# A hybrid encoder layer on one core: the second gate tile in another PSUM ring, the third weight in the extra staging tile, and block products with the summed index innermost

## The chip, the cores and the metric

The kernel runs on one core of a Trainium2 chip. The metric is the device time of one execution in microseconds. Before the change it is 937.7 us, the median of 3 runs (935.88 to 937.9). The core has a matrix engine (PE, with its weight loads shown apart as PEld), a vector engine (DVE), a scalar engine (ACT), GpSimd (POOL) and an engine that here only issues transfers (SP). Each engine works through its own list of instructions in order and waits where an operand isn't there yet.

## The reference

One layer on 512 tokens of width 1024. All inputs are float32.

```python
h = rms_norm(x, attn_norm_g[l])
(a_q, a_ckv, a_iq, a_ik, a_iw, s5_u, c_qkv, c_z, c_a, c_b,
 gates) = jnp.split(h @ w_in[l], split_points, axis=-1)
y_a = dsa_attention(...) @ w_proj_a[l]      # top-k sparse attention over a shared latent
y_b = s5_branch(...) @ w_proj_b[l]          # complex diagonal state space layer, then a GLU
y_c = gdn_branch(c_qkv, c_z, c_a, c_b, ...) @ w_proj_c[l]
g_a, g_b, g_c = jnp.split(jax.nn.sigmoid(gates), N_BRANCH, axis=-1)
x = x + (g_a * y_a + g_b * y_b + g_c * y_c) @ w_out[l]
x = x + conv_glu_ffn(rms_norm(x, ffn_norm_g[l]), w_up[l], ffn_conv_w[l], w_down[l])
return rms_norm(x, final_norm_g)
...
# in gated_delta_rule, in chunks of 64 tokens, 4 heads
m = jnp.where(strict, jnp.einsum('bhncd,bhnsd->bhncs', kb, k) * decay, 0.0)
rhs = jnp.concatenate([v * beta[..., None], kb * jnp.exp(gam)[..., None]], axis=-1)
sol = lax.linalg.triangular_solve(m + eye, rhs, left_side=True, lower=True, unit_diagonal=True)
```

The unit triangular system is solved per head and per chunk of 64 tokens.

## The kernel before

The input projection is cut into column tiles of 128, each an output of 128x512 (channels by tokens) summed over eight 128-row slices. Every float32 operand is split into a rounded part and its remainder, named h and l, and every slice is three matmuls: h by h, h by l and l by h. So one weight tile of 128x1024 feeds 24 matmuls of 128x512. A weight tile passes through three steps: a load into a staging tile w (SP, L280), a cast on ACT that makes wh (L256), and a subtraction on DVE that makes wl (L257). There are two normal staging tiles; a third one, w3, is there for some stretches, the start among them, and `wload` gives it to one load in three, by a counter `wi`.

PSUM is cut into rings of 128x512 tiles: "acc" has 2, "sm" 2, "pt" 3 and "po" 1. A matmul that starts a tile waits until the tile's former content has been read.

At the start the program loads x transposed (xt) in eight slices, splits it, and multiplies it by the first four weight tiles of the state space input: the first two into "acc", the other two into "pt". It also loads x as it is (sq) and sums its squares on ACT for the norm. Then h is scaled and split (hh, hl), and the projections follow in the order of a list. The first two gate tiles are made by `proj_pair`, slice by slice in turn, while h comes in slices; every gate is drained by a tanh on ACT (m_th, L1324) and sent to memory (gd, L1325).

The delta rule (`gdn_main`) makes for each head the matrix NT and inverts the unit triangular blocks of 64 as follows. The 32x32 diagonal blocks are sent through memory so that each of 128 partitions holds one block (g_ND, L942 to L946). The 16x16 diagonal blocks are inverted by substitution on DVE (L949, L950), and the off-diagonal 16x16 block is two products of 16x16 matrices: one with the off-diagonal part of g_ND, one with the inverse X2. Each product is four times a multiplication into a tile of 128x512 (L958) and a sum over its innermost index (L959). ACT and DVE copy the result into Xa and Ya (L961 to L968); these go to memory (g_xd, L972, L973) and come back as g_X (by SP) and g_Y (by POOL's queue, L980), block diagonal. PE multiplies g_X into g_NT; DVE masks the result into g_P (L998); PE multiplies that with g_Y, and so on for the other 32x32 halves.

The program is written stage by stage, with generators that let projections and stages take turns. The order of the instructions on each engine is set afterwards by a scheduler of the framework, from an estimate of its own; so a small edit can move instructions far from it. After the delta rule comes the sparse attention, the merge with the gates, the output projection and the gated MLP.

Of the kernel before, what the change touches and what calls it, by code (L numbers as in the profile page):

```python
# [13 lines left out]
OP = mybir.AluOpType  # L14
# [29 lines left out]
def _bc(ap, axis, n):  # L44
    a = ap.unsqueeze(axis)
    shape = list(a.shape)
    shape[axis] = n
    return a.broadcast_to(shape)
# [177 lines left out]
class _K:  # L226
# [46 lines left out]
    def wload(self, src, n=1024, hl=None, extra=False):  # L273
        nc = self.nc
        self.wi += 1
        if self.w3 and self.wi % 3 == 0:
            w = self.w3.tile([128, 1024], F32, tag="w3", name="w", bufs=1)
        else:
            w = self.wp.tile([128, 1024], F32, tag="w", name="w", bufs=2)
        nc.sync.dma_start(w[:, :n], src)  # L280
        if hl is None:
            if self.wx and extra:
                hl = [self.wx.tile([128, 1024], F32R, tag="x" + z, name="w" + z, bufs=1) for z in "hl"]
            else:
                hl = [self.wp.tile([128, 1024], F32R, tag="w" + z, name="w" + z, bufs=self.wb) for z in "hl"]
        h, l = hl
        if self.gpw and GP and self.wi % GP == 0:
            nc.scalar.copy(h[:, :n], w[:, :n])
            nc.gpsimd.tensor_tensor(l[:, :n], w[:, :n], h[:, :n].bitcast(F32), OP.subtract)
        else:  # L290
            self.split(h[:, :n], l[:, :n], w[:, :n])
        return h, l
# [57 lines left out]
    def proj_pair(self, i):  # L350

        self.ahead(2)
        two, pss = [self.fq.pop(0) for _ in range(2)], [self.acc(), self.acc()]
        assert [q[0] for q in two] == [i, i + 1]
        self.lasta, self.lastv = two[1][2:]
        for k in range(8):
            c = slice(k * 128, k * 128 + 128)
            for ps, q in zip(pss, two):
                wh, wl = q[1]
                self.mm(ps, wh[:, c], self.hh[:, k], k == 0, False)  # L360
                self.mm(ps, wl[:, c], self.hh[:, k], False, False)
                self.mm(ps, wh[:, c], self.hl[:, k], False, k == 7)
        self.ahead(3)
        return pss
# [451 lines left out]
    def gdn_main(self):  # L816
        nc = self.nc
        tt = nc.vector.tensor_tensor
# [36 lines left out]
        for h in range(4):  # L855
            for z, src in ((0, self.kT), (1, self.qT)):
                ps = self.gp()
                for t in range(4):
                    c = slice(t * 128, (t + 1) * 128)
                    self.tr(ps[:, c], src[:, h, c])  # L860
                dst = k_t[:, h]
                if z == 0:
                    nc.vector.tensor_copy(dst, ps)
                for t in range(4):
                    c = slice(t * 128, (t + 1) * 128)
                    jk = self.g2.tile([128, 128], F32, tag="jk", name="g_jk", bufs=2)
                    j = z * 16 + t * 4 + h
# [32 lines left out]
        for h in range(4):  # L900
            t2 = lambda nm: self.g2.tile([128, 512], F32, tag="t2", name="g_" + nm)
            p1, p2 = self.gp(), self.gp()
            for t in range(4):
                c = slice(t * 128, (t + 1) * 128)
# [3 lines left out]
            for i, x, y in ((h, self.kT, KB), (4 + h, self.qT, QD)):  # L908
# [4 lines left out]
                for t in range(4):  # L913
                    c = slice(t * 128, (t + 1) * 128)
# [10 lines left out]
            for t in range(4):  # L925
                c = slice(t * 128, (t + 1) * 128)
# [5 lines left out]
        lo, up, h0_, h1_ = slice(0, 64), slice(64, 128), slice(0, 16), slice(16, 32)  # L932
        ND = self.g2.tile([128, 2, 16, 16], F32, tag="t2", name="g_ND")
        W = self.g2.tile([128, 1024], F32, tag="S", name="g_W", bufs=1)
        w3 = lambda a, b, n: W[:, a:b].rearrange("p (i k) -> p i k", k=n)
        X, X2, X1, T1, X21 = w3(0, 256, 16), w3(256, 512, 16), w3(512, 640, 8), w3(640, 768, 8), w3(768, 896, 8)
        tmp = self.g2.tile([128, 512], F32, tag="t2", name="g_xt")
        Xa = self.g2.tile([128, 16, 32], F32, tag="t2", name="g_Xa")
        Ya = self.g2.tile([128, 16, 32], F32, tag="t2", name="g_Ya")
        nc.gpsimd.memset(Xa[lo, :, h1_], 0.0)  # L940
        nc.gpsimd.memset(Ya[up, :, h0_], 0.0)
        nc.sync.dma_start(ND[lo, 0], nv[:, h0_, h0_])  # L942
        nc.sync.dma_start(ND[up, 0], nv[:, h1_, h1_])
        nc.sync.dma_start(X.rearrange("p a b -> p (a b)"), self.I["const"][:, CC["eye16"][0]:CC["eye16"][1]])
        nc.sync.dma_start(ND[lo, 1], nv[:, h0_, h1_])
        nc.sync.dma_start(ND[up, 1], nv[:, h0_, h1_])  # L946
        for i in range(1, 16):
            tv = tmp[:, :i * i].rearrange("p (a b) -> p a b", a=i)
            tt(tv, X[:, 0:i, 0:i], _bc(ND[:, 0, 0:i, i], 2, i), OP.mult)  # L949
            nc.vector.tensor_reduce(X[:, i, 0:i], tv.rearrange("p j k -> p k j"), AX.X, OP.add)  # L950
        nc.vector.tensor_copy(X1[lo], X[lo, :, 0:8])
        nc.scalar.copy(X1[up], X[lo, :, 8:16])
        nc.scalar.copy(X2[lo], X[up])
        nc.scalar.copy(X2[up], X[up])
        t4 = tmp.rearrange("p (i k j) -> p i k j", i=4, k=8)
        for dst, a, b in ((T1, ND[:, 1].rearrange("p j i -> p i j"), X1), (X21, X2, T1)):
            for c in range(0, 16, 4):
                tt(t4, _bc(a[:, c:c + 4], 2, 8), _bc(b.rearrange("p j k -> p k j"), 1, 4), OP.mult)  # L958
                nc.vector.tensor_reduce(dst[:, c:c + 4], t4, AX.X, OP.add)  # L959
        tr_ = lambda x: x.rearrange("p i k -> p k i")  # L960
        nc.scalar.copy(Xa[lo, :, h0_], X[lo])  # L961
        nc.scalar.copy(Xa[up, :, h1_], X[up])
        nc.scalar.copy(Ya[lo, :, h0_], tr_(X[lo]))
        nc.scalar.copy(Ya[up, :, h1_], tr_(X[up]))
        nc.vector.tensor_copy(Xa[up, :, 0:8], X21[lo])
# [18 lines left out]
        for h0 in (0, 2):  # L984
# [5 lines left out]
            with self.tc.issue_after(self.lastm[2].ins):  # L990
                for h in range(2):
                    for t in range(4):
                        c = slice(t * 128, (t + 1) * 128)
# [7 lines left out]
            for h in range(2):  # L1001
                for t in range(4):
                    c = slice(t * 128, (t + 1) * 128)
# [38 lines left out]
        for t in range(4):  # L1042
            c = slice(t * 128, (t + 1) * 128)
# [40 lines left out]
        for h in range(4):  # L1084
# [3 lines left out]
            for t in range(4):  # L1088
                c = slice(t * 128, (t + 1) * 128)
# [608 lines left out]
```

## Time and profile before

| | |
|---|---|
| time, median of 3 runs | 937.7 us (935.88 to 937.9) |
| profiled execution | 937.33 us, its span 935.5 us |
| PE busy | 914.2 us, 98% of the span |
| DVE busy | 646.1 us, 69% |
| ACT busy | 414.4 us, 44% |
| mean granted clock of PE | 0.992 of full speed |
| data moved | 114.55 MB, 122 GB/s over the span |

The profiled execution is 0.37 us under the median. Busy PE means that a matmul is in flight; matmuls overlap, so the pace of a stretch is read from start to start and not from the duration of one. The granted clock is the share of 2.4 GHz that PE had; its other level is 1.2 GHz. A bracket at the end of a row of a timeline is the idle time of the engine before that instruction and what ended it.

### The profile page before, as it was taken

Reading aid. Unit: us, or ns where it says so; the run is one execution under the profiler, and the core shown is the slowest. Engines: PE = TensorE matmul, PEld = TensorE weight load, DVE = VectorE, ACT = ScalarE, POOL = GpSimd, SP = SyncE. Lnnn points to the kernel's source line nnn. Section 1 sums busy time; section 2 is a strip of 40 time slices with the busy share of each in tenths; the row PEclk is TensorE's granted clock in tenths of the full one; section 3 lists DMA queues with packets and bytes.
Section 4 is the critical chain, followed back from the end, with each engine's and each line's share of the span. In section 5 each row is a group of like instructions: output and inputs, shape, how many; then the busy total and the mean of one; then the engine's idle time right before and its main releaser. Section 6 shows DMA issues by size and latency. Waiting matters only on the chain.

```text
span 935.5 us, 12723 instructions
## 1 busy us (share of the span) xinstructions
PE 914.2 (98%) x4804; PEld 744.2 (80%) x4804; DVE 646.1 (69%) x1136; ACT 414.4 (44%) x753; POOL 62.7 (7%) x103
## 2 busy tenths in 40 slices
PE   8989999999999999899999999999999999999996
PEld 6768877788887778788777889888888888888885
DVE  6988498989999779467768545866666666522423
ACT  7467454244575634258733224534443443321212
POOL 3121001021003200400100000000000000000000
PEclk9999999999999999899999999999999999999999
DMA  9585323342335644631147513423223323232312
GB/s 341 179 208 150 105 95 114 119 147 90 101 103 136 166 119 150 191 124 37 45 135 234 205 46 113 136 90 110 94 90 100 103 90 94 87 113 91 103 55 90
DMA packets 48269, 114.55 MB, mean 122 GB/s; under 512 B 13712, under 2 KB 15120, under 8 KB 48080
## 3 DMA queue, kind: packets, MB, share of 16 engines
q1 hardware_dynamic: 40144, 96.76, 32.0%
q0 software_dynamic: 4032, 9.97, 4.4%
q10 hardware_dynamic: 4032, 7.01, 2.1%
q8 instruction: 38, 0.62, 0.3%
q14 instruction: 23, 0.19, 0.1%
HBM read 94.84 MB, written 14.42 MB: 117 GB/s over the span
## 4 chain that ended last, share of the span: by engine, by line
PE 84%; DVE 9%; issue 3%; DMA 2%; ACT 1%; SPq 1%; POOL 0%; POOLq 0%; DVEq 0%; ACTq 0%
PE ps_acc L248 43%; PE ps_sm L248 22%; PE ps_pt L248 13%; PE ps_po L248 4%; DVE wl L257 1%; PE ps_pt L251 1%; DMA sq<-in_x_dram 1%; PE ps_sm L251 1%; DMA w<-in_w_glu_dram 1%; DVE g_xt L958 1%; DVE g_W L959 1%; DVE a_p L1256 0%; DVE s_rd L710 0%; DVE ht L1491 0%; DVE hl L257 0%
## 5 line engine op out<-in xcount | busy, mean ns | idle before, releaser
L257 DVE TENSOR_TENSOR wl<-w,wh 128x1024 fp32r<-128x1024 f32 (+1 forms) x140 | 168.9, 1207 | 137.7 <-ACT wh L256 137.4
L256 ACT CAST wh<-w 128x1024 fp32r<-128x1024 f32 (+1 forms) x140 | 145.5, 1040 | 231.2 <-PE ps_acc L248 126.5
L248 PE MATMUL ps_acc<-hh,wh 128*128 128x512 f32 x376 | 151.2, 402 | 3.4 <-ACT m_th L1324 2.9
L248 PE MATMUL ps_acc<-hh,wl 128*128 128x512 f32 x376 | 150.4, 400 | 0.0
L248 PE MATMUL ps_acc<-hl,wh 128*128 128x512 f32 x376 | 149.2, 399 | 0.0
L248 PEld LDWEIGHTS ps_acc<-hh,wh 128*128 128x128 f32 x376 | 70.9, 188 | 21.4 <-ACT m_th L1324 3.3
L248 PEld LDWEIGHTS ps_acc<-hh,wl 128*128 128x128 f32 x376 | 71.0, 189 | 17.5 <-issue 1.2
L248 PEld LDWEIGHTS ps_acc<-hl,wh 128*128 128x128 f32 x376 | 70.9, 189 | 16.8 <-issue 1.1
L248 PE MATMUL ps_acc<-f_hh,wh 128*128 128x512 f32 x160 | 62.3, 389 | 0.0
L248 PE MATMUL ps_acc<-f_hl,wh 128*128 128x512 f32 x160 | 62.3, 389 | 0.0
L248 PE MATMUL ps_acc<-f_hh,wl 128*128 128x512 f32 x160 | 62.2, 389 | 0.0
L248 PE MATMUL ps_sm<-f_hh,wh 128*128 128x512 f32 x160 | 62.2, 389 | 0.0
L248 PE MATMUL ps_sm<-f_hl,wh 128*128 128x512 f32 x160 | 62.2, 389 | 0.0
L248 PE MATMUL ps_sm<-f_hh,wl 128*128 128x512 f32 x160 | 62.2, 389 | 0.0
L256 ACT CAST ah<-f_th 128x512 fp32r<-128x512 f32 x22 | 13.6, 620 | 57.6 <-DVE f_th L1629 57.6
L248 PEld LDWEIGHTS ps_sm<-f_hh,wh 128*128 128x128 f32 x160 | 30.1, 188 | 6.3
L248 PEld LDWEIGHTS ps_acc<-f_hl,wh 128*128 128x128 f32 x160 | 30.0, 188 | 6.3
L248 PEld LDWEIGHTS ps_sm<-f_hl,wh 128*128 128x128 f32 x160 | 30.0, 188 | 6.2
L248 PEld LDWEIGHTS ps_acc<-f_hh,wl 128*128 128x128 f32 x160 | 30.1, 188 | 6.2
L248 PEld LDWEIGHTS ps_acc<-f_hh,wh 128*128 128x128 f32 x160 | 30.0, 187 | 6.2
L248 PEld LDWEIGHTS ps_sm<-f_hh,wl 128*128 128x128 f32 x160 | 30.0, 187 | 6.2
L1627 ACT ACTIVATE f_th<-f_a 128x512 f32<-128x512 f32 x22 | 13.9, 632 | 45.2 <-DVE f_a L1624 45.2
(553 smaller groups left out, 1941.6 us busy)
## 6 DMA issues: line engine op xcount, KB each, us to landing
w<-in_w_in_dram SPq DMA_DIRECT2D x50, 512.0 KB, 3.5
w<-in_w_up_dram SPq DMA_DIRECT2D x44, 512.0 KB, 3.3
w<-in_w_down_dram SPq DMA_DIRECT2D x22, 512.0 KB, 3.3
gd<-m_th ACTq DMA_DIRECT2D x24, 256.0 KB, 2.1
m_th<-gd SPq DMA_DIRECT2D x24, 256.0 KB, 3.6
w<-in_w_out_dram SPq DMA_DIRECT2D x8, 512.0 KB, 3.9
sq<-in_x_dram SPq DMA_DIRECT2D x4, 512.0 KB, 9.0
w<-in_w_proj_b_dram SPq DMA_DIRECT2D x4, 512.0 KB, 3.8
```

The lines of the kernel that those rows point to most:

```text
L248: return self.nc.tensor.matmul(out, lhsT, rhs, start=start, stop=stop)
L251: return self.nc.tensor.transpose(out, in_, self.ident[base:base + n, base:base + n])
L256: self.lasta = nc.scalar.copy(hi, src)
L257: self.lastv = nc.vector.tensor_sub(lo, src, hi.bitcast(F32))
L958: tt(t4, _bc(a[:, c:c + 4], 2, 8), _bc(b.rearrange("p j k -> p k j"), 1, 4), OP.mult)
L959: nc.vector.tensor_reduce(dst[:, c:c + 4], t4, AX.X, OP.add)
L1627: nc.scalar.activation(th, tl[0], AF.Tanh)
```

## The change

There are three edits. `wload` gives the extra staging tile to the loads with `wi % 3 == 2` instead of 0. `proj_pair` takes its second tile from the "pt" ring. And the block products keep X1 and T1 transposed, with a transposed copy of the off-diagonal part of g_ND (NDt) that ACT makes in half of the tile Ya, so that both operands of each multiplication have the summed index innermost.

```diff
--- before.py
+++ after.py
@@ -273,7 +273,7 @@
     def wload(self, src, n=1024, hl=None, extra=False):
         nc = self.nc
         self.wi += 1
-        if self.w3 and self.wi % 3 == 0:
+        if self.w3 and self.wi % 3 == 2:
             w = self.w3.tile([128, 1024], F32, tag="w3", name="w", bufs=1)
         else:
             w = self.wp.tile([128, 1024], F32, tag="w", name="w", bufs=2)
@@ -350,7 +350,7 @@
     def proj_pair(self, i):
 
         self.ahead(2)
-        two, pss = [self.fq.pop(0) for _ in range(2)], [self.acc(), self.acc()]
+        two, pss = [self.fq.pop(0) for _ in range(2)], [self.acc(), self.acc("pt")]
         assert [q[0] for q in two] == [i, i + 1]
         self.lasta, self.lastv = two[1][2:]
         for k in range(8):
@@ -933,33 +933,37 @@
         ND = self.g2.tile([128, 2, 16, 16], F32, tag="t2", name="g_ND")
         W = self.g2.tile([128, 1024], F32, tag="S", name="g_W", bufs=1)
         w3 = lambda a, b, n: W[:, a:b].rearrange("p (i k) -> p i k", k=n)
-        X, X2, X1, T1, X21 = w3(0, 256, 16), w3(256, 512, 16), w3(512, 640, 8), w3(640, 768, 8), w3(768, 896, 8)
+        X, X2, X21 = w3(0, 256, 16), w3(256, 512, 16), w3(768, 896, 8)
+
+        X1, T1 = w3(512, 640, 16), w3(640, 768, 16)
         tmp = self.g2.tile([128, 512], F32, tag="t2", name="g_xt")
         Xa = self.g2.tile([128, 16, 32], F32, tag="t2", name="g_Xa")
         Ya = self.g2.tile([128, 16, 32], F32, tag="t2", name="g_Ya")
         nc.gpsimd.memset(Xa[lo, :, h1_], 0.0)
-        nc.gpsimd.memset(Ya[up, :, h0_], 0.0)
         nc.sync.dma_start(ND[lo, 0], nv[:, h0_, h0_])
         nc.sync.dma_start(ND[up, 0], nv[:, h1_, h1_])
         nc.sync.dma_start(X.rearrange("p a b -> p (a b)"), self.I["const"][:, CC["eye16"][0]:CC["eye16"][1]])
         nc.sync.dma_start(ND[lo, 1], nv[:, h0_, h1_])
         nc.sync.dma_start(ND[up, 1], nv[:, h0_, h1_])
+        NDt = Ya.rearrange("p (z a) b -> p z (a b)", z=2)[:, 0].rearrange("p (i j) -> p i j", i=16)
+        nc.scalar.copy(NDt, ND[:, 1].rearrange("p j i -> p i j"))
         for i in range(1, 16):
             tv = tmp[:, :i * i].rearrange("p (a b) -> p a b", a=i)
             tt(tv, X[:, 0:i, 0:i], _bc(ND[:, 0, 0:i, i], 2, i), OP.mult)
             nc.vector.tensor_reduce(X[:, i, 0:i], tv.rearrange("p j k -> p k j"), AX.X, OP.add)
-        nc.vector.tensor_copy(X1[lo], X[lo, :, 0:8])
-        nc.scalar.copy(X1[up], X[lo, :, 8:16])
+        tr_ = lambda x: x.rearrange("p i k -> p k i")
+        nc.vector.tensor_copy(X1[lo], tr_(X[lo, :, 0:8]))
+        nc.scalar.copy(X1[up], tr_(X[lo, :, 8:16]))
         nc.scalar.copy(X2[lo], X[up])
         nc.scalar.copy(X2[up], X[up])
         t4 = tmp.rearrange("p (i k j) -> p i k j", i=4, k=8)
-        for dst, a, b in ((T1, ND[:, 1].rearrange("p j i -> p i j"), X1), (X21, X2, T1)):
+        for dst, a, b in ((tr_(T1), NDt, X1), (X21, X2, T1)):
             for c in range(0, 16, 4):
-                tt(t4, _bc(a[:, c:c + 4], 2, 8), _bc(b.rearrange("p j k -> p k j"), 1, 4), OP.mult)
+                tt(t4, _bc(a[:, c:c + 4], 2, 8), _bc(b, 1, 4), OP.mult)
                 nc.vector.tensor_reduce(dst[:, c:c + 4], t4, AX.X, OP.add)
-        tr_ = lambda x: x.rearrange("p i k -> p k i")
         nc.scalar.copy(Xa[lo, :, h0_], X[lo])
         nc.scalar.copy(Xa[up, :, h1_], X[up])
+        nc.gpsimd.memset(Ya[up, :, h0_], 0.0)
         nc.scalar.copy(Ya[lo, :, h0_], tr_(X[lo]))
         nc.scalar.copy(Ya[up, :, h1_], tr_(X[up]))
         nc.vector.tensor_copy(Xa[up, :, 0:8], X21[lo])
```

On SP the edit of the staging tile moves a load. The rows are the start of the program; w is a weight tile, xt and sq are x transposed and plain. Before:

```order
L1424 DMA xt<-in_xt_dram 128x1024
L280 DMA w<-in_w_in_dram 128x1024
L1424 DMA xt<-in_xt_dram 128x1024 x2
L1432 DMA sq<-in_x_dram 128x1024 x3
L280 DMA w<-in_w_in_dram 128x1024
L1432 DMA sq<-in_x_dram 128x1024
L1455 DMA ident<-in_const_dram 128x128
L280 DMA w<-in_w_in_dram 128x1024
```

After:

```order
L1428 DMA xt<-in_xt_dram 128x1024
L280 DMA w<-in_w_in_dram 128x1024
L1428 DMA xt<-in_xt_dram 128x1024 x2
L280 DMA w<-in_w_in_dram 128x1024
L1436 DMA sq<-in_x_dram 128x1024 x4
L1459 DMA ident<-in_const_dram 128x128
L280 DMA w<-in_w_in_dram 128x1024
```

The second of these loads of w, the third weight of the program, stood behind three loads of sq and stands ahead of all four now.

On PE the matmuls of the first gates move. The rows are the start of the pair, right behind the last matmuls of the index projection; hh, hl and wh, wl are the parts of h and of the weights. Before:

```order
L248 MATMUL ps_sm<-xh,wl 76x512
L248 MATMUL ps_acc<-hh,wh 128x512
L248 MATMUL ps_acc<-hh,wl 128x512
L248 MATMUL ps_acc<-hh,wh 128x512
L248 MATMUL ps_acc<-hl,wh 128x512
L248 MATMUL ps_acc<-hh,wh 128x512
L248 MATMUL ps_acc<-hh,wl 128x512
L248 MATMUL ps_acc<-hl,wh 128x512
L248 MATMUL ps_acc<-hh,wh 128x512
L248 MATMUL ps_acc<-hh,wl 128x512
L248 MATMUL ps_acc<-hl,wh 128x512
L248 MATMUL ps_acc<-hh,wl 128x512
```

After:

```order
L248 MATMUL ps_sm<-xh,wl 76x512
L248 MATMUL ps_acc<-hh,wh 128x512
L248 MATMUL ps_pt<-hh,wh 128x512
L248 MATMUL ps_acc<-hh,wl 128x512
L248 MATMUL ps_acc<-hl,wh 128x512
L248 MATMUL ps_acc<-hh,wh 128x512
L248 MATMUL ps_acc<-hh,wl 128x512
L248 MATMUL ps_acc<-hl,wh 128x512
L248 MATMUL ps_acc<-hh,wh 128x512
L248 MATMUL ps_acc<-hh,wl 128x512
L248 MATMUL ps_pt<-hh,wl 128x512
L248 MATMUL ps_pt<-hl,wh 128x512
```

Two tiles of "acc" take turns before. Now one of the pair is in "pt", and further matmuls into "acc", those of the third gate, follow among them from the next rows on.

On PE the cover of the inverse moves too. The rows are around the first products with g_X; f is the output of the state space layer, a_c and a_wk belong to the attention's keys. Before:

```order
L248 MATMUL ps_pt<-f_l,wh 128x512
L248 MATMUL ps_pt<-f_h,wl 128x512
L248 MATMUL ps_acc<-a_ch,a_wkl 128x512
L248 MATMUL ps_acc<-wh,a_ch 128x512
L248 MATMUL ps_acc<-wl,a_ch 128x512
L248 MATMUL ps_acc<-wh,a_cl 128x512
L248 MATMUL ps_sm<-g_X,g_NT 128x64 x8
L248 MATMUL ps_acc<-f_h,wh 128x512
```

After:

```order
L248 MATMUL ps_pt<-f_h,wl 128x512
L248 MATMUL ps_acc<-a_ch,a_wkl 128x512
L248 MATMUL ps_sm<-g_X,g_NT 128x64 x3
L248 MATMUL ps_acc<-wh,a_ch 128x512
L248 MATMUL ps_sm<-g_X,g_NT 128x64 x2
L248 MATMUL ps_acc<-wl,a_ch 128x512
L248 MATMUL ps_acc<-wh,a_cl 128x512
L248 MATMUL ps_sm<-g_X,g_NT 128x64 x3
L248 MATMUL ps_pt<-a_kd,a_qh 128x128
L248 MATMUL ps_pt<-a_kl_3705,a_qh 128x128
L248 MATMUL ps_pt<-a_kd,a_qh 128x256
L248 MATMUL ps_pt<-a_kl_3705,a_qh 128x256
```

From the last matmul with g_rows up to the first one with g_X there are 198 matmuls before and 215 now, and the products with g_Y follow those with g_X after four score products, where twelve and more matmuls stood between them before.

On DVE the split of the attention's weight (a_wkl, L257) stood ahead of the copies into Xa and Ya that end the inverse, and stands behind them now.

## Rows read from the trace of the kernel before

**Rows 1.** The page: busy time of each engine; chain of waits, shares of the span.

```profile
PE 914.2 (98%) x4804; PEld 744.2 (80%) x4804; DVE 646.1 (69%) x1136; ACT 414.4 (44%) x753; POOL 62.7 (7%) x103
...
PE 84%; DVE 9%; issue 3%; DMA 2%; ACT 1%; SPq 1%; POOL 0%; POOLq 0%; DVEq 0%; ACTq 0%
```

**Rows 2.** Windows: length; busy (count) of PE, PEld, DVE, ACT, POOL; granted clock, DMA, GB/s.

```profile
50.00:60.00 10.00, 7.15 (x25) 5.35 (x24) 10.00 (x17) 4.36 (x5) 1.52 (x4) 0.83 1.10 247
270.00:280.00 10.00, 10.00 (x50) 8.20 (x50) 10.00 (x21) 5.93 (x29) 0.00 (x0) 1.00 0.30 97
380.00:390.00 10.00, 8.12 (x31) 7.27 (x32) 1.57 (x4) 2.15 (x5) 8.69 (x9) 0.66 0.81 207
```

**Rows 3.** Waits of PE: what it waited for: total us, times, longest us.

```profile
PE ps_acc L248 <- ACT m_th L1324: 2.9, 1, 2.9
PE ps_sm L248 <- DMA g_X<-g_xd: 2.4, 1, 2.4
...
PE ps_pt L248 <- DVE wl L257: 0.6, 1, 0.6
...
PE ps_acc L248 <- DVE wl L257: 0.4, 1, 0.4
```

**Rows 4.** Timeline of PE, third weight: start us, us, line, operation, operands [idle before].

```profile
20.27 0.40 PE L248 MATMUL ps_pt<-xh,wh 128*128 128x512 f32 x1
20.50 0.40 PE L248 MATMUL ps_pt<-xl,wh 128*128 128x512 f32 x1
21.48 0.50 PE L248 MATMUL ps_pt<-xh,wl 128*128 128x512 f32 x1 [0.58 <-DVE wl L257]
```

**Rows 5.** Timeline of PE, end of the gate pair and start of the third gate.

```profile
49.89 0.62 PE L248 MATMUL ps_acc<-hl,wh 128*128 128x512 f32 x2
53.37 0.50 PE L248 MATMUL ps_acc<-hh,wh 128*128 128x512 f32 x1 [2.85 <-ACT m_th L1324]
...
54.17 0.63 PE L248 MATMUL ps_acc<-hh,wh 128*128 128x512 f32 x1
...
57.58 0.39 PE L248 MATMUL ps_acc<-hh,wl 128*128 128x512 f32 x1
```

**Rows 6.** Timeline of ACT at the same place.

```profile
50.36 1.04 ACT L256 CAST wh<-w 128x1024 fp32r<-128x1024 f32 x1 [1.66 <-PE ps_acc L248]
51.42 1.28 ACT L1324 ACT_TABLE_LOAD   x1
52.72 0.60 ACT L1324 ACTIVATE m_th<-ps_acc 128x512 f32<-128x512 f32 x1
```

**Rows 7.** Timeline of DVE there: the split of the fourth gate's weight.

```profile
52.63 1.22 DVE L257 TENSOR_TENSOR wl<-w,wh 128x1024 fp32r<-128x1024 f32 x1
```

**Rows 8.** Timeline of PE, from the last decay row to the inverse.

```profile
332.16 0.50 PE L248 MATMUL ps_sm<-g_rows,rsel 40*128 40x512 f32 x1
...
379.10 0.39 PE L248 MATMUL ps_acc<-wh,a_cl 128*128 128x512 f32 x1
381.88 3.65 PE L248 MATMUL ps_sm<-g_X,g_NT 128*128 128x64 f32 x16 [2.39 <-DMA g_X<-g_xd]
385.28 0.77 PE L248 MATMUL ps_acc<-f_h,wh 128*128 128x512 f32 x1
...
388.77 0.40 PE L248 MATMUL ps_acc<-f_h,wl 128*128 128x512 f32 x1
```

**Rows 9.** Line L958, the block products: form, duration ns min/median/max, first and last start.

```profile
L958 DVE TENSOR_TENSOR g_xt<-g_ND,g_W x4: 1208/1216/1225, 355.4 to 362.3; 128x512 f32<-128x512 f32 x4
L958 DVE TENSOR_TENSOR g_xt<-g_W x4: 1160/1178/1205, 364.3 to 371.6; 128x512 f32<-128x512 f32 x4
```

**Rows 10.** Line L916, a DVE product of the same size, the same columns.

```profile
L916 DVE TENSOR_TENSOR g_KB<-g_k,g_er x4: 681/682/685, 305.0 to 332.0; 128x512 f32<-128x512 f32 x4
```

**Rows 11.** Timeline of DVE: the first product behind the inverse's matmuls.

```profile
385.56 0.76 DVE L998 TENSOR_TENSOR g_P<-ps_sm,cst 128x256 f32<-128x256 f32 x2 [5.67 <-PE ps_sm L248]
```

**Rows 12.** Timeline of PE, a rotation of the state space stage.

```profile
184.59 0.32 PE L248 MATMUL ps_po<-s_sr,s_ca 64*64 64x128 f32 x1 [0.92 <-DVE s_sr L715]
```

## The prediction

> **What bounds the kernel now.** I read the page first. PE is busy for 914.2 us, 98% of the span of 935.5 us, and holds 84% of the chain of waits [rows 1]. So an edit pays only where it removes a wait of PE, or the slow stretch behind one. The windows come next. Nearly all give a granted clock of 1.00; the two that fall clearly lower are 50 to 60 us (PE 7.15 of 10 us, clock 0.83) and 380 to 390 us (8.12, clock 0.66) [rows 2]. The waits of PE name the causes: 2.9 us once for the tanh of a gate (m_th, ACT, L1324) and 2.4 us once for the transfer of the inverse (g_X from g_xd) [rows 3]. A smaller one, 0.6 us, is for the split of a weight (wl, L257) [rows 3]. The timelines at these three places say what each costs. Fed at full clock, PE starts one 128x512 matmul each 0.23 us (20.27 to 20.50) [rows 4].
>
> **Prices of the three stalls.**
> - Third weight. From 20.50 to 21.48 is 0.98 us where 0.23 is the pace, so 0.75 us are lost [rows 4].
> - Gate pair. The row at 49.89 holds two matmuls, so the next was due at about 50.35 and starts at 53.37: 3.0 us lost [rows 5]. Behind it PE is slow: 54.17 to 57.58 are eight steps of 0.43 us [rows 5], which is the 1.2 GHz level beside the 0.23 us of 2.4 GHz, and the window's mean clock is 0.83 [rows 2]. Eight times 0.2 is 1.6 us, with 0.1 us for the step at 53.37: 4.7 us in all.
> - Inverse. The products with g_X were due at 379.10 + 0.23 = 379.33 and start at 381.88: 2.55 us [rows 8]. Their 16 matmuls then take 3.40 us to the next row at 385.28; by the ratio 0.43 to 0.23 they would take some 1.8 at full clock, 1.6 lost. From 385.28 to 388.77 are eight matmuls in 3.49 us instead of 1.84, another 1.65 [rows 8]. In all 5.8 us.
>
> Together the three hold 11.25 us.
>
> **Edit 1, the extra staging tile.** The third weight no longer waits for one of the two normal tiles. In the new order of SP it is loaded in front of the four loads of x instead of behind three of them, and DVE's split of it stands ahead of the start-up arithmetic. I take the whole 0.75 us off (bounds 0 and 0.9). What moves later by one weight load are the squares of x; their sum is wanted only for the scaling that comes after the matmuls of all four weights, so that costs nothing. Without this cover it would cost the time of one 512 KB load.
>
> **Edit 2, the second gate in the ring of three.** Now both tiles of the "acc" ring hold the pair, so the third gate's matmuls can't start until ACT has drained one of them. ACT at that time casts a weight (1.04 us), loads a table (1.28 us) and only then takes the tanh [rows 6]. With the second gate in "pt", the third gate has an "acc" tile free: the order of PE shows its matmuls in among the pair's, with nothing to wait for, since its weight was split long ago. What comes late next is the fourth gate's weight. Its split starts at 52.63 and lasts 1.22 us [rows 7], ready at 53.9. PE reaches it at 50.35 + 24 x 0.23 = 55.9, 2.0 us later. ACT's cast in front (50.36) keeps its place. So the whole 4.7 us goes (bounds 0 and 4.7), no wait in its place.
>
> **Edit 3, the block products.** Two things change. First the DVE: four products with g_ND take 1.216 us each, four without it 1.178 us [rows 9]. The same size with plain operands (L916) takes 0.682 us [rows 10]. In the old code the summed index strides through memory in one operand of each product, and in both in the first four; in the new code it is innermost in all. I take 0.68 us for the new form: 8 x (1.197 - 0.682) = 4.1 us less DVE chain (bounds 0 and 4.1). The price is one transposed copy on ACT of 128x256, at most a cast of four times the size (1.04 us) [rows 6].
> Second the order. Before, 198 matmuls stand between the last decay row (332.16) and the g_X products; in the new order I count 215, so PE has 17 x 0.23 = 3.9 us more of other work while the chain runs. One 128x512 split (a_wkl, about 0.68 us by the size in [rows 10]) also moves behind the copies that end the chain.
> Against it stand two places on ACT: the new copy waits for the transfer of g_ND and stands in front of a cast, and the copies into g_Ya now wait for the first four products, since the transposed factor lives in that tile, and a cast stands behind them too. Each can make a later weight split, and with it the DVE chain, late. I take 1.5 us together (bounds 0 and 3.5: a cast and a split at one of them, 1.04 + 1.22 [rows 6, 7], and one more split at the other).
> The sum from 332.16: before, g_X is due at +47.2 and lands at +49.7. After, it is due at 47.2 + 3.9 = +51.1 and lands at 49.7 - 4.1 - 0.6 + 1.5 = +46.5. The wait goes with 4.6 us in hand, and 2.6 if ACT costs all of 3.5. So the 5.8 us go (bounds 0 and 5.8).
> What is late next: before, twelve ordinary matmuls and more stand between the g_X products and those with g_Y and g_P. In the new order only four short score products do. DVE needs 0.76 us for the two g_P after PE's first result [rows 11], and g_Y still comes by POOL's queue. The nearest row of such a small wait of PE for DVE is 0.92 us in the state space stage, with no fall of the clock [rows 12]; I add 0.9 us (bounds 0, and 5.8 if it becomes a long one like that of g_X).
>
> **The rest.** The scheduler rearranges much of the program from about 60 us on, without adding work to PE. Such short waits as [rows 12] will come and go; I take nothing for them, and 3 us to either side. From 590 us on PE has one matmul behind the other, and no edit reaches there.
>
> **The sum.** 937.33 us of the profiled execution (its span of 935.5 and 1.8 around it) - 0.75 - 4.7 - 5.8 + 0.9 = 927.0. The median of the runs shown, 937.7, is 0.4 above that execution: 927.4 us.
>
> **Rivals.**
> 1. The wait moves to g_Y and g_P. For it: the cover between the two groups is gone, and the loads of g_Y come after those of g_X. Against it: g_X itself should land 4.6 us before it is wanted, and g_Y gains as much. If a long wait with a slow stretch returns, it takes back 5.8 - 0.9 = 4.9: 932.3 us.
> 2. The products don't get faster. Their 1.2 us could come from the two broadcast operands, which stay, and not from the strides. For it: the four with one strided operand take nearly as long (1.178) as those with two (1.216) [rows 9]. Against it: a broadcast operand is read no further apart than a plain one, which the strided ones are; but L916 has no broadcast, so that is argued and not seen. The chain is then 4.1 us longer, g_X lands at +50.6, just ahead of +51.1, and with ACT's bound 1.5 us late: 927.4 to 928.9, and 929 if a short slow stretch follows. The Trainium skill, "VectorE: DVE Perf Modes" (section on mode 1x), bears on this: it says the baseline mode takes fp32 and odd strides alike at one result per cycle. By that rule the new layout alone would gain nothing and the time would be this rival's; the trace has 1.2 us and 0.68 us for the same number of results [rows 9, 10], so something in the old operands halves the rate, and I hold it for the strides.
> 3. The gate stall isn't removed but moves to the fourth gate, because its split slips by more than the 2.0 us in hand. For it: DVE has no idle time from 50 to 60 us [rows 2]. Against it: in the new order one DVE row more stands ahead of that split. It gives back up to 4.7: 932.1 us.
> 4. Slower. DVE is full from 200 to 280 us (eight windows, one shown) while PE is full too [rows 2]. A weight feeds 24 matmuls, 5.5 us. If the new order puts more than 5.5 us of DVE work between two splits of weights in that stretch, PE waits at each of its 14 weights. At the 0.92 us of [rows 12] that makes 12.9 us, 940.3 us; it decides from 12 us on, some 0.9 us a weight. For it: the order of the top-k and state space work on DVE moves by several us there. Against it: the work isn't more, and before PE waited for splits 1.0 us in all [rows 3], so there is slack.
>
> **Chances.** Forecast 0.62 (924 to 931), rival 1 0.14, rival 2 0.06, rival 3 0.05, rival 4 0.09; 0.04 is left for 1 and 3 together with some short waits, 936.5 to 937.5, no change. A measurement here tells about 0.2%, 1.9 us, from no change. Faster is the forecast and rivals 1 to 3, less some of their upper ends: 0.83; the same 0.07; slower 0.10. The range is 922.5 (all three stalls gone, no new wait, 3 us of short waits gone) to 936 (rivals 1 and 3 nearly whole); outside lie rival 4 and a few in a hundred below.
>
> **What would show it.** Edit 1: no wait of PE for wl near 21 us. Edit 2: window 50 to 60 with PE at 10.00 and clock 1.00. Edit 3: products of 0.7 us, no wait for g_X, window of the g_X products at clock 1.00, and at most about 1 us before the g_Y products. It would be wrong if the chain of waits showed DVE splits between 200 and 280 us, or a new window with a clock well under 1.00.

## The result and the profile after

The changed kernel takes 924.53 us, the median of 4 runs (923.87 to 925.73), beside 937.14 us before (4 runs): a ratio of 0.9868, 95% interval 0.9851 to 0.9885, so 12.6 us less. The forecast was 927.4 us. The profiled execution after takes 924.56 us with a span of 922.8; before these were 937.33 and 935.5.

The same two lines of the page, PE's busy time and the chain of waits by engine:

```profile
PE 905.6 (98%) x4804; PEld 739.8 (80%) x4804; DVE 642.3 (70%) x1136; ACT 411.3 (45%) x752; POOL 63.1 (7%) x103
...
PE 89%; DVE 5%; DMA 2%; issue 2%; ACT 2%; SPq 0%; POOL 0%; POOLq 0%; DVEq 0%; ACTq 0%
```

PE does the same 4804 matmuls and still bounds the kernel; DVE's share of the chain is smaller than in [rows 1]. The busy time of PE falls by 8.6 us too. Matmuls at the lower clock are longer (0.63 us in [rows 5], 0.40 in [rows 4]); by the prediction's prices that is some 5 us of it, and the rest was not followed. The waits of PE, with the total, the count and the longest in us:

```profile
PE ps_po L248 <- DVE s_sr L715: 2.2, 2, 1.2
PE ps_po L248 <- POOL rB L1419: 1.5, 1, 1.5
PE ps_acc L248 <- ACT xh L259: 1.4, 1, 1.4
```

The two longest of [rows 3], for m_th and for g_X, are gone, and so are those for wl. What is now on top are short waits in the state space stage and at the start. The windows answer to [rows 2]; the second and third are those around the g_X products, which come earlier now:

```profile
50.00:60.00 10.00, 10.00 (x46) 7.94 (x46) 9.49 (x16) 7.28 (x12) 1.03 (x2) 1.00 1.11 238
...
360.00:370.00 10.00, 10.00 (x45) 8.19 (x45) 5.24 (x8) 2.67 (x4) 6.69 (x9) 1.00 0.82 219
370.00:380.00 10.00, 10.00 (x75) 8.86 (x74) 6.46 (x16) 4.84 (x10) 2.47 (x2) 1.00 0.60 169
```

No window of these has a granted clock under 1.00, and PE is busy throughout. The timeline of PE at the inverse, against [rows 8]:

```profile
319.86 0.49 PE L248 MATMUL ps_sm<-g_rows,rsel 40*128 40x512 f32 x1
...
370.12 0.40 PE L248 MATMUL ps_acc<-a_ch,a_wkl 128*128 128x512 f32 x1
370.35 0.78 PE L248 MATMUL ps_sm<-g_X,g_NT 128*128 128x64 f32 x6
...
373.17 0.28 PE L248 MATMUL ps_pt<-a_kl,a_qh 128*128 128x256 f32 x1
373.45 1.10 PE L248 MATMUL ps_sm<-g_Y,g_P 128*128 128x64 f32 x8
```

The first g_X product starts one step of 0.23 us behind the matmul ahead of it, and the g_Y products follow 0.28 us behind the last score product: no wait at either place. At the third weight, against [rows 4], PE steps evenly:

```profile
20.14 0.39 PE L248 MATMUL ps_pt<-xh,wh 128*128 128x512 f32 x1
20.37 0.40 PE L248 MATMUL ps_pt<-xl,wh 128*128 128x512 f32 x1
20.61 0.39 PE L248 MATMUL ps_pt<-xh,wl 128*128 128x512 f32 x1
```

The block products (line L962 now; duration in ns as min/median/max) answer to [rows 9]:

```profile
L962 DVE TENSOR_TENSOR g_xt<-g_Ya,g_W x4: 684/693/694, 343.2 to 348.6; 128x512 f32<-128x512 f32 x4
L962 DVE TENSOR_TENSOR g_xt<-g_W x4: 685/692/693, 350.0 to 355.7; 128x512 f32<-128x512 f32 x4
```

They take 0.693 us instead of 1.2, where 0.68 was forecast. So every sign that the prediction named has come. Whether the parts brought what they were credited with is what the experiments ask.

### The profile page after: what moved, and what is told of

It is laid out like the page before. It is cut to its first block, busy times and chain, and to the rows that moved or that the text cites. A ratio compares the mean times of both kernels' runs of the same rounds, so it can differ in the third digit from the quotient of the medians.

```text
span 922.8 us, 12725 instructions
## 1 busy us (share of the span) xinstructions
PE 905.6 (98%) x4804; PEld 739.8 (80%) x4804; DVE 642.3 (70%) x1136; ACT 411.3 (45%) x752; POOL 63.1 (7%) x103
## 4 chain that ended last, share of the span: by engine, by line
PE 89%; DVE 5%; DMA 2%; issue 2%; ACT 2%; SPq 0%; POOL 0%; POOLq 0%; DVEq 0%; ACTq 0%
PE ps_acc L248 47%; PE ps_sm L248 21%; PE ps_pt L248 14%; PE ps_po L248 4%; PE ps_pt L251 1%; PE ps_sm L251 1%; DMA w<-in_w_out_dram 1%; DVE wl L257 1%; DMA xt<-in_xt_dram 1%; DMA w<-in_w_glu_dram 1%; DVE a_p L1260 0%; ACT a_p L1262 0%; DVE g_o L1090 0%; DVE s_rd L710 0%; DVE a_wk L1139 0%
## 5 line engine op out<-in xcount | busy, mean ns | idle before, releaser
L257 DVE TENSOR_TENSOR wl<-w,wh 128x1024 fp32r<-128x1024 f32 (+1 forms) x140 | 169.3, 1210 | 136.6 <-ACT wh L256 134.6
L248 PE MATMUL ps_acc<-hh,wh 128*128 128x512 f32 x368 | 147.3, 401 | 0.0
L248 PE MATMUL ps_acc<-hh,wl 128*128 128x512 f32 x368 | 146.3, 398 | 0.0
L248 PE MATMUL ps_acc<-hl,wh 128*128 128x512 f32 x368 | 146.0, 397 | 0.0
L248 PEld LDWEIGHTS ps_acc<-hh,wl 128*128 128x128 f32 x368 | 69.0, 188 | 16.3 <-issue 0.4
```

What stands on the lines that cost most here:

```text
L248: return self.nc.tensor.matmul(out, lhsT, rhs, start=start, stop=stop)
L257: self.lastv = nc.vector.tensor_sub(lo, src, hi.bitcast(F32))
```

## The experiments

The three parts are named here the stage part (`wi % 3 == 2`), the gate part (`self.acc("pt")`) and the block part (all of the edits in `gdn_main`). The six mixed kernels are those that lie between the kernel before and the changed one. In the three series of experiments the kernel before took 937.28, 937.36 and 937.68 us, so a few tenths of a microsecond between series say nothing.

**The change without the block part.** The kernel before with

```diff
-        if self.w3 and self.wi % 3 == 0:
+        if self.w3 and self.wi % 3 == 2:
...
-        two, pss = [self.fq.pop(0) for _ in range(2)], [self.acc(), self.acc()]
+        two, pss = [self.fq.pop(0) for _ in range(2)], [self.acc(), self.acc("pt")]
```

> The change without its third part: gate tile in the ring of three and extra staging tile as in the changed kernel, block products strided as before. Its order has the same 215 matmuls ahead of the first g_X product as the changed kernel. Theory 'cover': the longer cover alone (17 matmuls, 3.9 us) is more than the 2.55 us wait of the kernel before, so no wait for g_X, granted clock 1.00 at the g_X products, and 924.5 to 925.5 us like the changed kernel, although the eight products take 1.2 us each. Theory 'products' (the 4.1 us of faster products are needed): a wait of 1 us or more for g_X with a slow stretch, 928 to 931 us.

Measured: 924.68 us (4 runs, 924.39 to 924.84; ratio to the kernel before 0.9863, 0.9848 to 0.9877), the time of the changed kernel. PE's order is, row for row, that of the changed kernel. Its trace, the line of the products, PE's timeline:

```profile
L958 DVE TENSOR_TENSOR g_xt<-g_ND,g_W x4: 1208/1218/1223, 342.5 to 349.4; 128x512 f32<-128x512 f32 x4
L958 DVE TENSOR_TENSOR g_xt<-g_W x4: 1184/1210/1235, 351.4 to 358.3; 128x512 f32<-128x512 f32 x4
```

```profile
320.83 0.49 PE L248 MATMUL ps_sm<-g_rows,rsel 40*128 40x512 f32 x1
...
371.32 0.78 PE L248 MATMUL ps_sm<-g_X,g_NT 128*128 128x64 f32 x6
```

The products are as slow as before and PE waits for nothing: g_X starts 50.5 us behind the last decay row, just as in the changed kernel. So 'cover' holds. The stall at the inverse went by the order alone, and the order came with the other two parts.

The order has two sides, though. PE asks for g_X later: 50.5 us behind the last decay row, where it was due at 47.2 before. And DVE's chain is shorter although its products are as slow. The last copy into Ya, in the kernel before and in this one:

```profile
376.51 0.28 DVE L968 COPY g_Ya<-g_W 64x128 f32<-64x128 f32 x1
```

```profile
362.19 0.28 DVE L968 COPY g_Ya<-g_W 64x128 f32<-64x128 f32 x1
```

That is 44.3 us behind the last decay row before (376.51 - 332.16) and 41.4 here: two updates of g_k (L809) and the split of a_wkl have left the chain, and no split in it waits for its cast. Little of this reaches g_X, whose last load lands 50.0 us behind the last decay row here and 50.6 before. PE's wait ended at 49.7 us before, and it asks at 50.5 now, so with the landing left as it was the later asking would be enough by itself.

**Each part alone.** The kernel before with one of the three: all of the edits in `gdn_main` for the block part, or one of the two lines above for each of the others.

> The third part alone: new layout of the block products, gate pair in the ring of two, third weight without the extra tile. 210 matmuls ahead of the first g_X product, 27 between the g_X and the g_Y products. Both theories: products 0.69 us, no wait for g_X, so the 5.8 us of the inverse go and the 4.7 us at the gates and the 0.75 us of the third weight stay: 930 to 931.5 us. If the gate's price were smaller than read from the timeline, it would come out nearer to 926.

Measured: 932.54 us (ratio 0.9951, 0.9939 to 0.9964), 4.7 us less than the 937.28 us of the kernel before in those runs; 1 us above the top of the forecast. The waits for g_X and its slow stretch are gone, but the order brings new short waits. Two of them stand in the first and the third of these rows of PE; the second is the last decay row, the fourth the first g_X products:

```profile
163.83 1.05 PE L248 MATMUL ps_pt<-s_U,s_wt 64*64 64x128 f32 x14 [0.92 <-DVE s_yy L747]
...
334.06 0.50 PE L248 MATMUL ps_sm<-g_rows,rsel 40*128 40x512 f32 x1
...
381.44 0.50 PE L248 MATMUL ps_acc<-f_h,wh 128*128 128x512 f32 x1 [0.68 <-ACT a_V L1228]
...
384.35 1.95 PE L248 MATMUL ps_sm<-g_X,g_NT 128*128 128x64 f32 x16
```

The block products are fast here, and DVE's last copy into Ya still comes late:

```profile
L962 DVE TENSOR_TENSOR g_xt<-g_Ya,g_W x4: 684/692/693, 358.4 to 363.7; 128x512 f32<-128x512 f32 x4
L962 DVE TENSOR_TENSOR g_xt<-g_W x4: 684/688/693, 365.2 to 373.8; 128x512 f32<-128x512 f32 x4
```

```profile
378.17 0.28 DVE L972 COPY g_Ya<-g_W 64x128 f32<-64x128 f32 x1
```

That is 44.1 us behind the last decay row (378.17 - 334.06), only 0.2 us earlier than in the kernel before, where the products take 1.2 us. The last load of g_X lands at 50.2 us, and PE asks for it at 50.3. So here too the wait went by a longer cover, 12 matmuls in this order, and not by the products.

> The second part alone: second gate tile in the ring of three, strided block products, third weight without the extra tile. 215 matmuls ahead of the first g_X product. Theory 'cover': gate wait (4.7) and inverse wait (5.8 and the 0.5 for a split beside it) both gone, only the 0.75 us of the third weight stay: 925 to 926.5 us. Theory 'products': only the 4.7 us go, 932 to 933 us.

Measured: 926.69 us (ratio 0.9885, 0.9872 to 0.9898), 10.6 us less: 'cover', with 0.2 us over its upper end.

> The first part alone: extra staging tile for the third weight, gate pair in the ring of two, strided products. 215 matmuls ahead of the first g_X product here too. Theory 'cover': the 0.75 us and the 5.8 us of the inverse go, the 4.7 us at the gates stay: 929.5 to 931 us. Theory 'products': only 0.75 us go, 936 to 937 us.

Measured: 929.17 us (ratio 0.9912, 0.9898 to 0.9927), 8.1 us less: 'cover', 0.3 us under its lower end. The gate stall stands in its trace just as in [rows 5]:

```profile
49.13 0.62 PE L248 MATMUL ps_acc<-hl,wh 128*128 128x512 f32 x2
52.61 0.50 PE L248 MATMUL ps_acc<-hh,wh 128*128 128x512 f32 x1 [2.85 <-ACT m_th L1324]
```

**Each part taken out.** The changed kernel with the gate part undone, and with the stage part undone:

```diff
-        two, pss = [self.fq.pop(0) for _ in range(2)], [self.acc(), self.acc("pt")]
+        two, pss = [self.fq.pop(0) for _ in range(2)], [self.acc(), self.acc()]
```

```diff
-        if self.w3 and self.wi % 3 == 2:
+        if self.w3 and self.wi % 3 == 0:
```

> The changed kernel with the gate pair put back into the ring of two. The wait for the tanh and its slow stretch return (3.0 + 1.7 us), the rest stays: 929 to 929.5 us. If the second part's gain was mostly the order that it brings about, and not the wait: under 927 us.

Measured: 930.72 us, 6.2 us above the changed kernel and 1.2 us above the top of the forecast. The 2.85 us wait for m_th is back. The rest stands at the very start of the profiled execution: a wait of 2.54 us for xh (1.36 in the changed kernel), and behind it a window with the lower clock:

```profile
10.00:20.00 10.00, 8.80 (x31) 6.90 (x32) 8.66 (x32) 9.40 (x13) 4.29 (x2) 0.83 1.03 416
```

PE's order is, row for row, that of the stage part alone, and all of the 2.2 us by which this profile is longer than that one stand before 15 us. So the gate stall has the same price in both. The start differs between the kept profiles: the wait for xh is 0.6 to 2.5 us, and this window is at 0.83 in five of the fourteen and at 1.00 in the others. Whether the edits have a part in that was not tried.

> The changed kernel without the extra staging tile for the third weight. By the 0.75 us of the timeline: 925.3 us. By what the second part alone lay above the second and the first together (926.7 against 924.7): 926.5 us.

Measured: 926.43 us, 1.9 us above the changed kernel: the second number. The timeline shows a second wait beside that of [rows 4], at the index scores; the first row is this kernel's, the second that of the gate part alone, which lacks the stage part too:

```profile
93.36 0.47 PE L248 MATMUL ps_sm<-ikh,a_iq 128*128 128x512 f32 x1 [0.56 <-DMA a_iq<-sp_l]
```

```profile
95.34 0.47 PE L248 MATMUL ps_sm<-ikh,a_iq 128*128 128x512 f32 x1 [0.96 <-ACT wh L256]
```

The gate part alone has no wait at 21 us: its start is late and partly at the lower clock (the window 10 to 20 us at 0.83), so PE comes to the third weight only at 22.9 us.

**The sum from these.** The gate part is worth 4.5 us beside the stage part (929.17 - 924.68), the stage part 2.0 beside the gate part (926.69 - 924.68). With both there are 12.6 us to explain (937.28 - 924.68), so 6.1 us are left, which either part brings alone and both together bring once. This is one subtraction and can't test itself: that the stage part alone comes to 2.0 + 6.1 and the gate part alone to 4.5 + 6.1 follows from it.

The traces give a test. The stage part alone keeps the gate stall, and at many places of its program PE has done the very same matmuls as in the kernel before. Two such places are these, ahead of the inverse and behind it. Before:

```profile
374.34 0.39 PE L248 MATMUL ps_pt<-f_h,wl 128*128 128x512 f32 x1
...
471.25 0.50 PE L248 MATMUL ps_acc<-g_ol,wh 128*128 128x512 f32 x1
```

With the stage part alone:

```profile
371.48 0.39 PE L248 MATMUL ps_pt<-f_h,wl 128*128 128x512 f32 x1
...
462.76 0.50 PE L248 MATMUL ps_acc<-g_ol,wh 128*128 128x512 f32 x1
```

It is 2.86 us ahead at the first place and 8.49 at the second: 5.6 us for the inverse, where [rows 8] gave 5.8. Of the 2.86 us, 0.74 stand right behind the third weight (21.31 against 22.05 us for the same matmul). The other 2.1 came between 66 and 330 us, with the new order and the new staging, where the prediction had looked for nothing.

**One strided operand.** The changed kernel without the transposed copy:

```diff
-        nc.scalar.copy(NDt, ND[:, 1].rearrange("p j i -> p i j"))
...
-        for dst, a, b in ((tr_(T1), NDt, X1), (X21, X2, T1)):
+        for dst, a, b in ((tr_(T1), ND[:, 1].rearrange("p j i -> p i j"), X1), (X21, X2, T1)):
```

> The changed kernel without the transposed copy: in the first four products one operand is strided, the other has its summed index innermost; the last four are as changed. Same order of PE. If one strided operand costs as much as two: first four 1.18 to 1.22 us, last four 0.69 us. If it takes two for the slow rate: all 0.7 us. The time is 924.5 us in either case, since the products are off the path by more than their 2 us.

Measured: 925.14 us (924.2 to 926.5), no different. The products:

```profile
L960 DVE TENSOR_TENSOR g_xt<-g_ND,g_W x4: 1055/1070/1073, 342.4 to 348.9; 128x512 f32<-128x512 f32 x4
L960 DVE TENSOR_TENSOR g_xt<-g_W x4: 692/692/693, 350.7 to 356.1; 128x512 f32<-128x512 f32 x4
```

With the first operand strided the product takes 1.07 us, 0.38 more than without; neither of my two answers was right. Both forms have the same broadcasts, so it is the stride that is slow. (In the kernels with the old products, the last four have a stride in the second operand alone, a shorter one, and take 1.18 us [rows 9] to 1.21; why that is slower was not tried.)

**A longer way for the factors.** Does the block part, which brings no time, at least bring something in hand? Both kernels got a further copy through memory ahead of the loads of g_X and g_Y:

```diff
+        xe = self.dp.tile([2, 4, 16, 32, 32], F32, tag="xe", name="g_xe", bufs=1)
+        for z in range(2):
+            nc.sync.dma_start(xe[z], xd[z])
+        xd = xe
```

> The changed kernel with one more transfer in the way of the inverse: g_xd is copied to a second place in memory, and g_X and g_Y are loaded from there. This should make g_X land some 2.5 to 3 us later. Its order has 216 matmuls ahead of the first g_X product. Theory 'reserve' (the faster products brought no time but some 3 us in hand): the copy uses up what is in hand and little more, a wait for g_X under 1 us, 924.5 to 926 us. Theory 'nothing in hand': a wait of 2.5 us with a slow stretch behind it, 929 to 931 us.

Measured: 925.69 us (924.63 to 926.48). PE waits neither for g_X nor for g_Y.

> The same second copy in the kernel without the third part of the change (strided products, gate tile and staging tile as changed); 215 matmuls ahead of the first g_X product. Theory 'reserve': here g_X landed less than 1 us ahead of PE, so a wait of 1.5 to 2.5 us for g_X appears and with it a stretch at the lower clock like that of the kernel before: 927.5 to 930.5 us, 3 to 5 us above the changed kernel with the same copy. If the products' speed gives no reserve, both kernels with the copy take the same time.

Measured: 932.78 us (928.78 to 933.34), 7.1 us above the other. In the profiled execution the long wait is for g_Y, not g_X; two of the matmuls behind it show the lower clock, at steps of 0.43 us:

```profile
379.39 1.08 PE L248 MATMUL ps_sm<-g_Y,g_P 128*128 128x64 f32 x8 [3.43 <-DMA g_Y<-g_xe]
...
381.98 0.63 PE L248 MATMUL ps_acc<-f_l,wh 128*128 128x512 f32 x1
382.41 0.63 PE L248 MATMUL ps_acc<-f_h,wl 128*128 128x512 f32 x1
```

Its window 380 to 390 us has a granted clock of 0.66, as in [rows 2]. But the pair doesn't settle the reserve: with the copy, the changed kernel's order puts 14 matmuls of 128x512 between the g_X and the g_Y products and the other's only three. So I repeated it with a copy for g_Y alone, where PE's order is the same in both, row for row:

```diff
+        xe = self.dp.tile([4, 16, 32, 32], F32, tag="xe", name="g_xe", bufs=1)
+        nc.sync.dma_start(xe, xd[1])
+        xd = [xd[0], xe]
```

> The changed kernel with one more copy through memory for the factor of g_Y alone, so that g_Y lands some 3 us later. PE's order is that of the changed kernel (215 matmuls ahead of g_X, three between g_X and g_Y). Theory 'reserve': the chain of the inverse ends early enough that the copy is just covered, a wait for g_Y under 1 us, 924.5 to 926 us. If nothing is in hand for g_Y: a wait of 2 to 3 us and a stretch at the lower clock, 929 to 931 us.

> The same copy for g_Y in the kernel without the third part (strided products), with the same order of PE, row for row. Theory 'reserve': its loads of g_X and g_Y are issued 2 to 3 us later than in the changed kernel (counted from the last decay row), so the copy isn't covered: a wait for g_Y of 1 to 3 us and a slow stretch, 927 to 932 us, 2 to 6 us above the changed kernel with the same copy. If the third part gives no reserve, both take the same.

Measured: 928.62 us (927.96 to 930.5) and 928.91 us (925.75 to 929.32): no difference, and the changed kernel was not under 926 us as I had expected. Its profile, a wait for g_Y and a slow window:

```profile
375.36 1.63 PE L248 MATMUL ps_sm<-g_Y,g_P 128*128 128x64 f32 x8 [1.53 <-DMA g_Y<-g_xe]
```

```profile
370.00:380.00 10.00, 8.46 (x48) 7.43 (x47) 4.70 (x14) 3.80 (x9) 6.02 (x5) 0.78 0.70 203
```

In the other kernel the profiled execution was its fastest, 925.75 us; it waited 1.38 us for g_X, and the clock did not fall there. So the two profiles show what the block part has in hand (g_X is waited for without it and not with it), but not what 3 us more do to the time. For g_Y hardly anything is left of it: its loads are issued 1.9 us earlier with the block part (the first 47.2 us behind the last decay row, against 49.1), but the last lands only 0.4 us earlier (55.0 against 55.4). The theory, as I had put numbers on it, fell.

**Both gate tiles in the ring of three.** The changed kernel with `[self.acc("pt"), self.acc("pt")]`.

> The changed kernel with both gate tiles in the ring of three, which leaves both tiles of the ring of two for the gates that follow. If any of the changed kernel's time still hangs on the gates' tiles, 0.5 to 1 us less; the timeline of the changed kernel shows no wait there, so I expect 924.5 us, within 0.5 us.

Measured: 924.17 us (924.01 to 926.59), the same. Nothing more hangs on the gates' tiles, and no kernel here is told from the changed one as faster.

## Why the prediction was right, and where its working was not

The forecast took 10.3 us off the profiled execution; 12.8 us went (937.33 - 924.56). By its terms:

**Gate pair, 4.7 us.** Right: 4.5 us by the runs without the block part. The 6.2 us with it have the difference at the start in them. The slow stretch behind a wait has to be counted with the wait; the wait alone is 2.85 us.

**Third weight, 0.75 us (bounds 0 and 0.9).** The wait at 21 us went as said, and its size held where two profiles can be laid side by side (0.74 us). The whole edit brings more, 1.9 to 2.0 us by the two pairs of runs, above the upper bound. The kernels without this part show a second wait at the index scores, 0.56 and 0.96 us, that those with it don't have; that the counter, which goes on through the program, moves the staging of a later weight as well is only argued. The slow start of one profile has a part in it too, so the rest of this term stays open.

**Inverse, 5.8 us.** The size was right (5.6 us from the rows of two traces) and the cause was wrong. The prediction put it under the third edit, as a sum of faster products (4.1 us) and a longer cover (3.9 us). The cover was enough, and it needs no third edit. It came with the first edit alone and with the second alone, since the scheduler orders the whole program anew after each. The third edit alone brings a cover of its own, of 12 matmuls.

**The DVE chain, 4.1 us shorter.** Beside the kernel before, the chain of the changed kernel is 4.0 us shorter, from the last decay row to the last copy into Ya (44.3 and 40.4 us); the prediction's terms make 3.2 (4.1 + 0.6 - 1.5). That they are near is luck. The order alone brings 3.0 us, where the prediction had 0.6 for one split, and the products bring 1.0. This is the difference to the kernel without the block part, which has the same order on PE: 40.4 us (360.22 - 319.86) against 41.4 (362.19 - 320.83), though its products take 4.2 us longer (8 x 0.52). The rows of DVE in the changed kernel show where the rest stayed:

```profile
328.89 1.23 DVE L257 TENSOR_TENSOR wl<-w,wh 128x1024 fp32r<-128x1024 f32 x1 [0.40 <-DMA g_ND<-g_nd]
...
334.49 1.23 DVE L257 TENSOR_TENSOR wl<-w,wh 128x1024 fp32r<-128x1024 f32 x1 [0.77 <-ACT wh L256]
...
356.90 1.23 DVE L257 TENSOR_TENSOR wl<-w,wh 128x1024 fp32r<-128x1024 f32 x1 [0.46 <-ACT wh L256]
...
360.22 0.28 DVE L972 COPY g_Ya<-g_W 64x128 f32<-64x128 f32 x1
```

The splits of the weights stand in DVE's order among the products, and most wait for their casts, which come when PE has finished with a weight. Four such waits, with one for a transfer and one for a copy, make 2.3 us from the start of the substitution on; the other kernel has none there. One more update of g_k (L809, 0.68 us) stands in this chain too. 4.2 - 2.3 - 0.7 is 1.2, against the 1.0 that was measured. The prediction had 1.5 us for two places on ACT; it had not seen that a faster chain runs into the pace of PE's weights, so that time saved ahead of a split is given back at the split.

The loads of g_X come earlier by more than the chain does. SP's issues of them, in the changed kernel and in the one without the block part:

```profile
L984 SPq DMA_DIRECT2D g_X<-g_xd x4: 325/480/487, 362.2 to 363.7; - x4
```

```profile
L980 SPq DMA_DIRECT2D g_X<-g_xd x4: 325/496/1238, 365.4 to 367.6; - x4
```

From the last decay row these are 42.4 to 43.8 us against 44.6 to 46.8, in part because the writes of Xa and Ya ahead of them land after 2.3 us in the one and 3.2 to 3.5 in the other; why was not followed. The last load lands at 47.5 us against 50.0, and PE asks at 50.5 in both: 3.0 us in hand, where the prediction had 4.6, and 0.5 without the block part.

**The new wait of 0.9 us before the g_Y products.** It did not come: PE goes from the score products to g_Y without a break. DVE had g_P ready while the score products ran, and g_Y had landed. These 0.9 us, and some 2 us won between 66 and 330 us, for which the prediction took nothing, make up the 2.9 us between 927.4 and 924.5; the 2 us are read from the stage part alone.

**The rivals.** The wait for g_Y (rival 1) is not in the changed kernel, but the kernel with a longer way for both factors and without the block part shows it, 3.43 us and a window at 0.66. Slow products by broadcast (rival 2) fell: the broadcasts are still there and the products take 0.693 us, 1.07 with one stride put back. The time that it was given, 927.4 us and more, was wrong besides: with products of 1.2 us the kernel takes 924.68. The Trainium skill, "VectorE: DVE Perf Modes" (section on mode 1x), says that strides work in this mode and gives the mode one result per cycle, with no price for a stride. The prediction read it as a rule by which the new layout gains nothing; these runs show a price, and they decide. The fourth gate's weight (rival 3) was in time, since PE is full from 50 to 60 us (10.00, clock 1.00). The waits for splits between 200 and 280 us (rival 4) did not come: no wl is among the waits of PE.

## What to carry to other kernels

In a program that a scheduler orders, a gain that shows where an edit was made need not come from that edit: build each edit alone and the whole without it, and compare the orders first. A part that is left over from a subtraction is not measured until rows of two traces show it in one place. An operation made faster in the middle of an in-order queue can give its time back at the next instruction of that queue that waits for someone else, as the products did here, so read what stands between it and the end of the chain. And price a stall of a clocked engine with the slow stretch behind it: here that was a third of the gate's price and more than half of the inverse's.

## What was not expected of the hardware

The clock did not fall behind every wait of like length. With a copy for g_Y, a wait of 1.53 us went with a window at 0.78 in the one kernel; in the other, waits of 1.38 and 0.38 us left the same window at 1.00, though PE was busy for 8.25 us of it, against 8.46. At the start a wait of 2.40 us left PE at full clock, in the change without the block part, and one of 2.07 us, in the gate part alone, went with the window at 0.83:

```profile
10.64 0.51 PE L248 MATMUL ps_acc<-xh,wh 128*128 128x512 f32 x1 [2.40 <-ACT xh L259]
```

```profile
10.48 0.50 PE L248 MATMUL ps_acc<-xh,wh 128*128 128x512 f32 x1 [2.07 <-ACT xh L259]
```

So the length of one wait didn't settle it here. The four executions of the kernel with the 1.38 us lie between 925.75 and 929.32 us; whether the clock parts them was not seen, since only the fastest was profiled.

A DVE product of 128x512 in float32 takes 0.693 us with the summed index innermost in both operands. It takes 1.07 us with the first operand read at a distance of 64 bytes, 1.18 to 1.21 with the second at a distance of 32 bytes, and 1.22 to 1.25 with both (medians of the kernels).
